# GpSimd's folds, sums and weight splits go to VectorE, and the norms around matrix multiplications are rebuilt

## The chip, the core and the metric

The kernel runs on one core of a Trainium2 chip. The metric is the time of one execution on the device in microseconds: the median of several runs. The profile is taken from one execution by the hardware profiler. TensorE (PE) multiplies matrices, VectorE (DVE) and ScalarE (ACT) work on elements, GpSimd (POOL) as well, and SyncE (SP) issues the DMAs of the weights.

## The reference

Three blocks work on one sequence of 256 tokens of width 1024, with 16 further tokens ahead of them in the first block. All arithmetic is float32.

```
h = concat([meta, x])                                  # 272 tokens
for i in range(2):                                     # first block
    f1 = swiglu(rmsnorm(h, g0), gate, up, down)
    h = h + 0.5 * rmsnorm(f1, g1)
    hn = rmsnorm(h, g2)
    m = neighborhood_attention(hn) if i == 0 else diff_attention(hn)
    h = h + rmsnorm(m, g3)
    f2 = swiglu(rmsnorm(h, g4), gate, up, down)
    h = h + 0.5 * rmsnorm(f2, g5)
h = h[:, 16:]                                          # second block
proj = rms_norm(h, g) @ w_in                           # u_pool, u_lru, u_gate
y = concat([pool_mixer(u_pool), rg_lru(conv(u_lru)) * gelu(u_gate)])
h = h + y @ w_out
h = h + square(relu(rms_norm(h, g) @ w_up)) @ w_down
h = h + sigmoid(rms_norm(h, g) @ w_ple_gate + b) * (p @ w_ple_proj)
h = rms_norm(h, g)
# third block: adaptive norm, short conv and window attention, w_out, then peer_ffn
# (16384 experts, top 16 of 8 heads) added to the stream
```

`rmsnorm(x, g)` is `x * rsqrt(mean(x*x) + 1e-6) * g`.

## The kernel before

The stream `h` lies with features on partitions: 8 tiles of 128 features, each with N = 272 or 256 columns of tokens. A float32 multiplication is made of three passes: each weight block and each input is split into a high part (`hi`, `zh`, `ah`: ACT, L66 and L269) and the rest (`lo`, `zl`, `al`: a subtraction), and TensorE adds hi·high, lo·high and hi·rest (L181, L182, L186).

Weights come in blocks of 128x1024. `Stream.use` hands the next block to a multiplication and splits the blocks that are to come: two ahead, three in the first part. A flag `gp` in the plan says whether VectorE or GpSimd makes `lo` (L67). GpSimd has the flag for most blocks of the mixing block (`w_in_2`, gates, pool, `w_ple_proj_2`, the first half of `w_out_2`) and for some of the third block.

`gemm_it` runs the outputs in groups of four tiles. For each group it goes over K in chunks of two tiles, 24 matmuls each, accumulating in PSUM banks: one bank for each output at N = 272, one for two outputs at N = 256. `evac` takes a group out of PSUM.

A norm is a sum over partitions: squares of 8 tiles are folded into one (`sq`), a matmul with a column of ones sums it (`ss_add`, L214), ACT and VectorE make the reciprocal root (`nsd`, `nv`, `ny`: `ss_chain`, `root`), and a matmul with the identity spreads it over all partitions (`ss_spread`, L244). There are two kinds.

- Behind a projection (`proj_post_it`): its output is squared and scaled by the gain (`fg`), and `update` adds `fg` times the spread root to `h` (tiles `ut`, two at a time from the third on, the add on GpSimd, L326).
- Ahead of a multiplication (`z_tile`, `z_after`): the input is split without its root, and the root is multiplied into the outputs of the multiplication, so its sum may come while the first group runs. `z_tile` makes `zh`, `zl` and the squares of two tiles and lets GpSimd fold them (L276, L278).

`update` and `z_tile` are called from the multiplication itself as its inputs come due. Each engine works its instructions off in the order in which they are issued here. The mixing block (`mixer_2`) runs its elementwise work from a generator that `gemm_it` steps once per chunk (`self.step`), beside the multiplications. The last stage, `peer`, streams 256 blocks of expert tables and keeps its GpSimd work.

Of the kernel before, what the change touches and what calls it, by code (L numbers as in the profile page):

```python
# [86 lines left out]
class Kern:  # L87
# [57 lines left out]
    def gemm_it(self, name, KT, groups, N, rhs, evac, after=None, tail=None):  # L145
# [3 lines left out]

        nc = self.nc  # L150
        per_bank = 1 if N > 256 else 2
        pending = None
        for og, g in enumerate(groups):
# [3 lines left out]
            else:  # L157
                banks = [self.bank2() for _ in range((g + 1) // 2)]
                outs = [banks[o // 2][:, o % 2] for o in range(g)]
            per = 8 // g  # L160
            for kc in range(0, KT, per):
# [4 lines left out]
                if pending is not None and kc:  # L166
                    next(after, None)
                    evac(*pending)
                    pending = None
                if after is not None and og == 0 and end:  # L170
                    next(after)
                order = [(k2, o) for k2 in range(min(per, KT - kc)) for o in range(g)]
                if kc and end:
                    order.sort(key=lambda x: (x[1] // per_bank, x[0], x[1]))
                late = []
                for n, (k2, o) in enumerate(order):
# [3 lines left out]
                    first = kt == 0 and (N > 256 or o % 2 == 0)  # L180
# [7 lines left out]
                    if tail is not None and end and og == len(groups) - 1 and (n + 1) * g % len(order) == 0:  # L188
                        b = (n + 1) * g // len(order) - 1
                        if (b + 1) % per_bank == 0:  # L190
                            tail(b // per_bank, outs)
                yield
            if og == 0 and after is not None:
                next(after)
# [8 lines left out]
    def gemm(self, *args, **kw):  # L203
        for _ in self.gemm_it(*args, **kw):
            pass

# [41 lines left out]
    def ss_rows(self, ss, N):  # L248
        return self.ss_spread(ss, self.ss_chain(ss, N), N)
# [12 lines left out]
    def z_tile(self, kt, g, c0, N):  # L262

        nc, gp = self.nc, self.nc.gpsimd
# [10 lines left out]
        if kt:  # L275
            gp.tensor_tensor(sq[:, 0:2, :N], sq[:, 0:2, :N], sq[:, p, :N], op=OP.add)  # L276
        if kt == 6:
            gp.tensor_tensor(sq[:, 0, :N], sq[:, 0, :N], sq[:, 1, :N], op=OP.add)  # L278

    def z_after(self, N):  # L280
# [3 lines left out]
        def after():  # L284
            yield
# [24 lines left out]
    def update(self, g, c0, N):  # L310
# [4 lines left out]
        def add(kt):  # L315
# [6 lines left out]
            else:  # L322
# [3 lines left out]
                self.nc.gpsimd.tensor_tensor(hk, hk, t, op=OP.add)  # L326
# [18 lines left out]
    def proj_post_it(self, name, KT, rhs, N, gpost, bias=None):  # L345

        nc, gp = self.nc, self.nc.gpsimd
# [5 lines left out]
        def piece(og, b, outs):  # L353
            per = 1 if N > 256 else 2
            for o in range(per * b, per * b + per):
                kt = 4 * og + o
                nc.scalar.activation(sq[:, kt, :N], outs[o], AF.Square,  # L357
                                     **({} if bias is None else {"bias": bias(kt)}))
            for o in range(per * b, per * b + per):
                kt = 4 * og + o  # L360
                if kt == 6 and N > 256:
# [1456 lines left out]
```

## Time and profile before

| | |
|---|---|
| median of 3 runs | 2502.68 us (2500.74 to 2504.39) |
| the profiled execution | 2512.54 us |
| its span | 2510.8 us |
| TensorE busy | 2366.9 us |
| VectorE busy | 1862.3 us |
| ScalarE busy | 1133.1 us |
| GpSimd busy | 516.6 us, of it 228.6 in the last stage (L1472) and 162.7 for `lo` (L67) |

The span is from the first to the last instruction on the core. Busy time is the time in which at least one instruction of the engine runs; matmuls overlap. The view of the cores gives the mean clock that TensorE was granted, where 1.00 is 2.4 GHz and 0.50 is 1.2 GHz, its two levels.

### The profile page before, as it was taken

How to read it: one execution, taken by the hardware profiler on the slowest of the kernel's cores; microseconds unless marked ns; L12 is line 12 of the kernel's file. 1: busy time of each engine (PE TensorE's matmuls, PEld its weight loads, DVE VectorE, ACT ScalarE, POOL GpSimd, SP SyncE). 2: the span in 40 equal slices, each digit the busy share in tenths (PEclk: the TensorE clock that was granted, in tenths of full speed). 3: DMA queues.
4: the chain of work that ended last, by engine and by line, in shares of the span. 5: the costliest groups of instructions: out<-in, count | busy, mean ns of one | idle time of the engine just before them, and what ended most of it. 6: DMA issues, size and time to landing. Idle time of an engine off the chain costs nothing.

```text
span 2510.8 us, 47982 instructions
## 1 busy us (share of the span) xinstructions
PE 2366.9 (94%) x19988; PEld 2296.5 (91%) x19988; DVE 1862.3 (74%) x2769; ACT 1133.1 (45%) x1509; POOL 516.6 (21%) x302
## 2 busy tenths in 40 slices
PE   8998998998999998998799989999889999899999
PEld 8998878998999978998789988999889999889999
DVE  7776657676776767777976565578989999999554
ACT  5444544444444454444555455454433334333443
POOL 0002002002001112003510015024445554553000
PEclk9998989998999988998899989899899999999999
DMA  6575414565557413666356543355444444444554
GB/s 216 176 248 200 164 51 133 184 227 178 176 192 266 147 64 126 201 230 203 114 168 204 194 152 123 128 177 185 146 141 152 152 150 153 143 135 152 187 188 147
DMA packets 114950, 418.79 MB, mean 167 GB/s; under 512 B 13086, under 2 KB 14382, under 8 KB 113708
## 3 DMA queue, kind: packets, MB, share of 16 engines
q1 hardware_dynamic: 113356, 406.46, 48.8%
q0 software_dynamic: 1376, 9.26, 1.0%
q8 instruction: 156, 2.56, 0.4%
q14 instruction: 62, 0.51, 0.1%
HBM read 414.62 MB, written 1.05 MB: 166 GB/s over the span
## 4 chain that ended last, share of the span: by engine, by line
PE 71%; DVE 18%; issue 4%; ACT 3%; POOL 2%; DMA 2%; DVEq 0%; SPq 0%; ACTq 0%; POOLq 0%
PE b L181 18%; PE b L186 17%; PE b L182 17%; DVE lo L67 5%; PE b L1555 4%; PE b L1553 4%; PE b L1554 4%; DVE zl L271 2%; DVE G L124 1%; DVE ob L1474 1%; ACT hi L66 1%; DMA raw<-in_dn 1%; PE b L1491 1%; DVE e L124 1%; PE b L214 1%
## 5 line engine op out<-in xcount | busy, mean ns | idle before, releaser
L67 DVE TENSOR_TENSOR lo<-raw,hi 128x1024 fp32r<-128x1024 f32 x658 | 895.9, 1371 | 421.3 <-ACT hi L66 420.3
L66 ACT ACTIVATE hi<-raw 128x1024 fp32r<-128x1024 f32 x722 | 754.8, 1056 | 841.1 <-PE b L186 412.4
L181 PE MATMUL b<-zh,hi 128*128 128x256 f32 (+1 forms) x3504 | 1013.0, 289 | 20.1 <-ACT zh L269 10.1
L182 PE MATMUL b<-zh,lo 128*128 128x256 f32 (+1 forms) x3504 | 1004.0, 287 | 17.6 <-DVE lo L67 13.5
L186 PE MATMUL b<-zl,hi 128*128 128x256 f32 (+1 forms) x3504 | 996.2, 286 | 14.6 <-DVE zl L271 14.6
L181 PEld LDWEIGHTS b<-zh,hi 128*128 128x128 f32 x3504 | 676.2, 193 | 28.5 <-ACT zh L269 11.3
L182 PEld LDWEIGHTS b<-zh,lo 128*128 128x128 f32 x3504 | 677.8, 193 | 20.1 <-DVE lo L67 14.8
L186 PEld LDWEIGHTS b<-zl,hi 128*128 128x128 f32 x3504 | 671.8, 193 | 17.4 <-DVE zl L271 17.3
L1555 PE MATMUL b<-zh,lo 128*128 128x256 f32 x1024 | 292.9, 286 | 2.6 <-DVE lo L67 2.6
L1553 PE MATMUL b<-zh,hi 128*128 128x256 f32 x1024 | 294.3, 287 | 0.0
L1554 PE MATMUL b<-zl,hi 128*128 128x256 f32 x1024 | 289.1, 282 | 0.0
L1472 POOL TENSOR_TENSOR oa<-e,gt 128x768 bf16<-128x768 bf16 x128 | 228.6, 1786 | 223.6 <-DVE e L124 196.9
L182 PE MATMUL b<-ah,lo 128*128 128x272 f32 (+1 forms) x960 | 271.1, 283 | 3.0 <-DVE lo L67 2.8
L181 PE MATMUL b<-ah,hi 128*128 128x272 f32 (+1 forms) x960 | 270.4, 282 | 0.0
L186 PE MATMUL b<-al,hi 128*128 128x272 f32 (+1 forms) x960 | 268.5, 282 | 0.0
L67 POOL TENSOR_TENSOR lo<-raw,hi 128x1024 fp32r<-128x1024 f32 x64 | 162.7, 2549 | 253.5 <-ACT hi L66 238.2
L1555 PEld LDWEIGHTS b<-zh,lo 128*128 128x128 f32 x1024 | 194.7, 190 | 6.5 <-DVE lo L67 4.6
L372 POOL TENSOR_TENSOR sq<-sq 128x272 f32<-128x272 f32 (+2 forms) x20 | 25.7, 1286 | 843.1 <-ACT sq L357 842.5
L1554 PEld LDWEIGHTS b<-zl,hi 128*128 128x128 f32 x1024 | 197.8, 193 | 0.0
L1553 PEld LDWEIGHTS b<-zh,hi 128*128 128x128 f32 x1024 | 195.0, 190 | 0.0
L182 PEld LDWEIGHTS b<-ah,lo 128*128 128x128 f32 x960 | 180.7, 188 | 4.4 <-DVE lo L67 4.4
L181 PEld LDWEIGHTS b<-ah,hi 128*128 128x128 f32 x960 | 180.7, 188 | 0.0
(374 smaller groups left out, 2663.2 us busy)
## 6 DMA issues: line engine op xcount, KB each, us to landing
raw<-in_gu SPq DMA_DIRECT2D x176, 512.0 KB, 4.2
raw<-in_peer_u SPq DMA_DIRECT2D x128, 512.0 KB, 3.3
raw<-in_peer_v SPq DMA_DIRECT2D x128, 512.0 KB, 3.3
raw<-in_dn SPq DMA_DIRECT2D x88, 512.0 KB, 4.7
raw<-in_w_adaT SPq DMA_DIRECT2D x48, 512.0 KB, 4.6
raw<-in_w_up SPq DMA_DIRECT2D x32, 512.0 KB, 4.2
raw<-in_w_down SPq DMA_DIRECT2D x32, 512.0 KB, 3.3
raw<-in_w_in SPq DMA_DIRECT2D x30, 512.0 KB, 3.4
```

What stands on the lines that cost most here:

```text
L66: nc.scalar.activation(hi[:, :width], raw, AF.Copy)
L67: (nc.gpsimd if gp else nc.vector).tensor_tensor(lo[:, :width], raw, hi[:, :width].bitcast(FT), op=OP.subtract)
L124: self.nc.vector.tensor_tensor(out, a, b, op=op)
L181: nc.tensor.matmul(outs[o], hi[:, w], xh, start=first, stop=False, skip_group_check=True)
L182: nc.tensor.matmul(outs[o], lo[:, w], xh, start=False, stop=False, skip_group_check=True)
L186: nc.tensor.matmul(out, a, b, start=False, stop=kt == KT - 1, skip_group_check=True)
L271: nc.vector.scalar_tensor_tensor(self.zl[:, k, :N], self.h[:, k, c0:c0 + N], self.gcol(g, k), self.zh[:, k, :N].bitcast(FT), op0=OP.mult, ...
L372: gp.tensor_tensor(sq[:, 0:w, :N], sq[:, 0:w, :N], sq[:, n:n + w, :N], op=OP.add)
L1472: nc.gpsimd.tensor_tensor(oa, e.unsqueeze(2).to_broadcast([128, 4, 3, 64]), gt[:, t0:t0 + 4].unsqueeze(3).to_broadcast([128, 4, 3, 64]), o ...
L1553: nc.tensor.matmul(dst, hi[:, w], ah[:, a], start=first, stop=False, skip_group_check=True)
L1554: nc.tensor.matmul(dst, hi[:, w], al[:, a], start=False, stop=False, skip_group_check=True)
L1555: nc.tensor.matmul(dst, lo[:, w], ah[:, a], start=False, stop=last, skip_group_check=True)
```

## The change

GpSimd is left with memsets, DMAs and its part of the last stage. The folds, the adds to `h`, the scaling of `e0` and all flagged splits ahead of the last stage are VectorE's. Besides:

- `z_tile` folds once, behind the last pair of tiles.
- `z_after`: the sum and root go from the end of the first group to the second chunk of the second group; the spread, and with it the first group's evacuation, to the chunk behind that.
- `proj_post_it`: each output is squared and folded as it is finished; the last output of a 256-column projection has a bank of its own; only two sums are made (tiles 0 and 7); the scalings of the last four outputs stand behind the sums.
- `warm(n)` issues n multiplications of the identity, read as bfloat16, into a bank that nobody reads: 6, 9 and 10 around the sums of a projection, 9 and 11 at two later norms (the second block's last and the third block's second). There are 190 in all.

```diff
     def gemm_it(...)
+                if tail is not None and og == len(groups) - 1:
+                    outs[g - 1] = self.bank()[:, :N]
...
                 if pending is not None and kc:
                     next(after, None)
-                    evac(*pending)
-                    pending = None
-                if after is not None and og == 0 and end:
-                    next(after)
+                    if kc >= 2 * per:
+                        evac(*pending)
+                        pending = None
...
             if og == 0 and after is not None:
-                next(after)
...
+    def warm(self, n):
+
+        b, x = self.bank(), self.ident.bitcast(BF)
+        for _ in range(n):
+            self.nc.tensor.matmul(b[:, :256], x[:, :128], x, start=True, stop=True)
...
     def ss_rows(self, ss, N):
-        return self.ss_spread(ss, self.ss_chain(ss, N), N)
+        y = self.ss_chain(ss, N)
+        self.warm(9)
+        rb = self.ss_spread(ss, y, N)
+        self.warm(11)
+        return rb
...
     def z_tile(self, kt, g, c0, N):
-        if kt:
-            gp.tensor_tensor(sq[:, 0:2, :N], sq[:, 0:2, :N], sq[:, p, :N], op=OP.add)
         if kt == 6:
-            gp.tensor_tensor(sq[:, 0, :N], sq[:, 0, :N], sq[:, 1, :N], op=OP.add)
+            for n in (2, 4, 6):
+                self.tt(sq[:, 0:2, :N], sq[:, 0:2, :N], sq[:, n:n + 2, :N], OP.add)
+            self.tt(sq[:, 0, :N], sq[:, 0, :N], sq[:, 1, :N], OP.add)
...
     def update(self, g, c0, N):
-                self.nc.gpsimd.tensor_tensor(hk, hk, t, op=OP.add)
+                self.tt(hk, hk, t, OP.add)
...
     def proj_post_it(self, name, KT, rhs, N, gpost, bias=None):
+        def tail(o, outs):
+            square(4 + o, outs[o])
+            if o < 3:
+                self.tt(sq[:, 0, :N], sq[:, 0, :N], sq[:, 4 + o, :N], OP.add)
             else:
-                st["ss"] = self.bank()
-                sums(0)
-                if N <= 256:
-                    sums(1), sums(6)
-                sums(7, True)
+                st["outs"] = outs
...
         yield from self.gemm_it(name, KT, [4, 4], N, rhs, evac, tail=tail)
-        self.rb = self.ss_rows(st["ss"], N)
+        outs = st["outs"]
+        self.warm(6)
+        ss = self.bank()
+        self.ss_add(ss, sq[:, 0, :N], N, True, False)
+        self.ss_add(ss, sq[:, 7, :N], N, False, True)
+        for o in range(2):
+            scaled(4 + o, outs[o])
+        y = self.ss_chain(ss, N)
+        for o in range(2, 4):
+            scaled(4 + o, outs[o])
+        self.warm(9)
+        self.rb = self.ss_spread(ss, y, N)
+        self.warm(10)
...
-                        nc.gpsimd.tensor_scalar(e0[:, j], e0[:, j], c[:, 0, j:j + 1], None, op0=OP.mult)
+                        nc.vector.tensor_scalar(e0[:, j], e0[:, j], c[:, 0, j:j + 1], None, op0=OP.mult)
...
-            gp = lambda i: True
-            add("w_in_2", 0, 4), add("w_in_2", 4, 5, gp=gp), add("gates_2", gp=gp), add("w_in_2", 9, gp=gp)
-            add("pool_2", gp=gp), add("w_ple_proj_2", gp=gp), add("w_out_2", gp=lambda i: i < 4)
+            add("w_in_2", 0, 4), add("w_in_2", 4, 6), add("gates_2"), add("w_in_2", 10)
+            add("pool_2"), add("w_ple_proj_2"), add("w_out_2")
```

VectorE's order at the first norm behind a projection (end of the first feed-forward part; `sq` folds, `fg` scalings, `nv` to `ny` the root, `ut` and `h` the update), before:

```order
L67 TENSOR_TENSOR lo<-raw,hi 128x1024 x3
L364 TENSOR_SCALAR fg<-b,vh 128x272 x2
L124 TENSOR_TENSOR sq<-sq 128x272
L364 TENSOR_SCALAR fg<-b,vh 128x272 x2
L236 TENSOR_SCALAR nv<-b 128x3
L225 RECIPROCAL ny<-nsd 128x3
L226 SCALAR_TENSOR_TENSOR na<-ny 128x3
L124 TENSOR_TENSOR na<-na,nv 128x3
L228 SCALAR_TENSOR_TENSOR ny<-na,ny 128x3
L124 TENSOR_TENSOR ut_2519<-fg,b 128x272
```

and now:

```order
L67 TENSOR_TENSOR lo<-raw,hi 128x1024 x3
L124 TENSOR_TENSOR sq<-sq 128x272 x3
L372 TENSOR_SCALAR fg<-b,vh 128x272 x2
L247 TENSOR_SCALAR nv<-b 128x3
L236 RECIPROCAL ny<-nsd 128x3
L237 SCALAR_TENSOR_TENSOR na<-ny 128x3
L124 TENSOR_TENSOR na<-na,nv 128x3
L239 SCALAR_TENSOR_TENSOR ny<-na,ny 128x3
L372 TENSOR_SCALAR fg<-b,vh 128x272 x2
L124 TENSOR_TENSOR ut_2547<-fg,b 128x272
L124 TENSOR_TENSOR h<-h,ut_2547 128x272
L124 TENSOR_TENSOR ut_2547<-fg,b 128x272
```

The three folds stand together, the scalings stand around the root's chain instead of ahead of it, and both adds to `h` follow `ut`.

VectorE's order a little later, where the next multiplication's fourth pair of tiles is split (`zl`) and the sum of its norm comes (`nv`), before:

```order
L271 SCALAR_TENSOR_TENSOR zl<-h,vt,zh 128x272 x2
L67 TENSOR_TENSOR lo<-raw,hi 128x1024
L271 SCALAR_TENSOR_TENSOR zl<-h,vt,zh 128x272 x2
L67 TENSOR_TENSOR lo<-raw,hi 128x1024 x2
L236 TENSOR_SCALAR nv<-b 128x3
L225 RECIPROCAL ny<-nsd 128x3
```

and now:

```order
L286 SCALAR_TENSOR_TENSOR zl<-h,vt,zh 128x272 x2
L67 TENSOR_TENSOR lo<-raw,hi 128x1024
L286 SCALAR_TENSOR_TENSOR zl<-h,vt,zh 128x272 x2
L124 TENSOR_TENSOR sq<-sq 128x544 x3
L124 TENSOR_TENSOR sq<-sq 128x272
L67 TENSOR_TENSOR lo<-raw,hi 128x1024 x4
L247 TENSOR_SCALAR nv<-b 128x3
L236 RECIPROCAL ny<-nsd 128x3
```

The folds are VectorE's, and four blocks' `lo` now stand ahead of `nv`, where there were two.

VectorE's order in the mixing block, from the root of its norm (`ul`, `up` are the projected parts, `xb` the convolution, `xl` the rest of its split), before:

```order
L124 TENSOR_TENSOR na<-na,nv 128x2
L228 SCALAR_TENSOR_TENSOR ny<-na,ny 128x2
L124 TENSOR_TENSOR ul<-b,r 128x2x256 x2
L970 SCALAR_TENSOR_TENSOR xb<-ul,vt,xb 128x256 x6
L124 TENSOR_TENSOR xl<-xb,xh 128x512
L970 SCALAR_TENSOR_TENSOR xb<-ul,vt,xb 128x256 x6
L124 TENSOR_TENSOR up<-b,r 128x2x256 x2
L124 TENSOR_TENSOR xl<-xb,xh 128x512
L124 TENSOR_TENSOR p_12880<-up 128x4x270
```

and now (from the same instruction):

```order
L124 TENSOR_TENSOR na<-na,nv 128x2
L239 SCALAR_TENSOR_TENSOR ny<-na,ny 128x2
L67 TENSOR_TENSOR lo<-raw,hi 128x1024
L124 TENSOR_TENSOR ul<-b,r 128x2x256 x2
L975 SCALAR_TENSOR_TENSOR xb<-ul,vt,xb 128x256 x6
L67 TENSOR_TENSOR lo<-raw,hi 128x1024
L124 TENSOR_TENSOR up<-b,r 128x2x256 x2
L124 TENSOR_TENSOR xl<-xb,xh 128x512
L975 SCALAR_TENSOR_TENSOR xb<-ul,vt,xb 128x256 x6
L67 TENSOR_TENSOR lo<-raw,hi 128x1024
L124 TENSOR_TENSOR xl<-xb,xh 128x512
```

The blocks' `lo` stand between the mixing work, which had none of them on this engine.

## Rows read from the trace of the kernel before

**Rows 1.** The page, part 1: busy us, share of span, instructions.

```profile
PE 2366.9 (94%) x19988; PEld 2296.5 (91%) x19988; DVE 1862.3 (74%) x2769; ACT 1133.1 (45%) x1509; POOL 516.6 (21%) x302
```

**Rows 2.** The view of the cores.

```profile
core 0: 2510.8 us, clock 0.960
```

**Rows 3.** TensorE's waits: for what, us in total, times, longest.

```profile
PE b L182 <- DVE lo L67: 17.2, 12, 4.6
PE b L186 <- DVE zl L271: 14.6, 13, 2.1
PE b L244 <- DVE ny L228: 12.3, 8, 3.6
```

**Rows 4.** TensorE's timeline, first norm (start, us, instruction, idle before).

```profile
208.84 0.29 PE L186 MATMUL b<-al,hi 128*128 128x272 f32 x1
210.51 1.66 PE L214 MATMUL b<-ones,sq 128*128 128x1 f32 x12 [1.39 <-DVE sq L124]
213.39 1.46 PE L244 MATMUL b<-ident,ny 128*128 128x128 f32 x6 [1.22 <-DVE ny L228]
216.41 0.59 PE L181 MATMUL b<-zh,hi 128*128 128x272 f32 x1 [1.56 <-ACT zh L269]
...
217.26 0.43 PE L182 MATMUL b<-zh,lo 128*128 128x272 f32 x1
217.48 0.43 PE L181 MATMUL b<-zh,hi 128*128 128x272 f32 x1
...
235.20 0.92 PE L214 MATMUL b<-ones,sq 128*128 128x1 f32 x6
```

**Rows 5.** VectorE's timeline, the same norm.

```profile
210.02 0.44 DVE L124 TENSOR_TENSOR sq<-sq 128x272 f32<-128x272 f32 x1 [0.68 <-POOL sq L372]
...
213.17 0.16 DVE L228 SCALAR_TENSOR_TENSOR ny<-na,ny 128x3 f32<-128x3 f32 x1
214.89 0.44 DVE L124 TENSOR_TENSOR ut<-fg,b 128x272 f32<-128x272 f32 x1 [1.56 <-PE b L244]
...
217.17 2.00 DVE L271 SCALAR_TENSOR_TENSOR zl<-h,vt,zh 128x272 fp32r<-128x272 f32 x2
...
226.53 2.38 DVE L67 TENSOR_TENSOR lo<-raw,hi 128x1024 fp32r<-128x1024 f32 x1
```

**Rows 6.** GpSimd's timeline, the same norm.

```profile
217.34 1.53 POOL L326 TENSOR_TENSOR h<-h,ut 128x544 f32<-128x544 f32 x1 [5.68 <-DVE ut L124]
```

**Rows 7.** Line L271 on VectorE, 971.75 to 973.2: ns min/median/max.

```profile
L271 DVE SCALAR_TENSOR_TENSOR zl<-h,vt,zh x2: 478/992/1507, 971.4 to 971.8; 128x256 fp32r<-128x256 f32 x2
```

**Rows 8.** Windows: length; busy us of PE, PEld, DVE, ACT, POOL; clock; DMA share; GB/s.

```profile
211.70:222.00 10.30, 7.52 (x34) 7.33 (x35) 7.77 (x16) 4.82 (x10) 3.65 (x3) 0.50 0.55 214
228.70:232.20 3.50, 1.46 (x9) 1.25 (x10) 3.50 (x4) 1.02 (x2) 2.25 (x2) 1.00 0.49 150
235.60:310.00 74.40, 74.40 (x551) 69.04 (x550) 45.83 (x107) 41.44 (x79) 0.57 (x1) 1.00 0.49 164
1172.00:1262.00 90.00, 66.87 (x477) 64.55 (x476) 79.69 (x89) 44.52 (x68) 49.01 (x23) 0.85 0.29 97
```

**Rows 9.** TensorE's timeline, the norm before the mixing block.

```profile
1166.06 3.58 PE L214 MATMUL b<-ones,sq 128*128 128x1 f32 x16 [4.13 <-POOL sq L372]
```

**Rows 10.** VectorE by form, 260 to 290.

```profile
L67 DVE TENSOR_TENSOR lo<-raw,hi 128x1024 fp32r<-128x1024 f32 x9 | 10.9, 1225 | 11.8 <-ACT hi L66 11.8
```

**Rows 11.** VectorE by form, mixing block, 1172 to 1262.

```profile
L271 DVE SCALAR_TENSOR_TENSOR zl<-h,vt,zh 128x256 fp32r<-128x256 f32 x8 | 9.4, 1211 | 0.3 <-ACT zh L269 0.3
...
L1000 DVE SCALAR_TENSOR_TENSOR rr<-th,rr 128x512 f32<-128x512 f32 x2 | 5.5, 2744 | 0.1
...
L228 DVE SCALAR_TENSOR_TENSOR ny<-na,ny 128x2 f32<-128x2 f32 x1 | 2.3, 2259 | 0.0
...
L1020 DVE SCALAR_TENSOR_TENSOR t<-t,rr 128x512 f32<-128x512 f32 x2 | 1.4, 688 | 0.7 <-ACT t L1018 0.7
```

**Rows 12.** GpSimd by form, the same stretch.

```profile
L67 POOL TENSOR_TENSOR lo<-raw,hi 128x1024 fp32r<-128x1024 f32 x15 | 37.6, 2521 | 31.3 <-ACT hi L66 31.3
```

More of the change, by code (lines that the diff above doesn't have):

```diff
@@ L159, in gemm_it @@
                 outs = [banks[o // 2][:, o % 2] for o in range(g)]
+                if tail is not None and og == len(groups) - 1:
+                    outs[g - 1] = self.bank()[:, :N]
+            unit = {}
+            for o in range(g):
+                alone = N > 256 or tail is not None and og == len(groups) - 1 and o >= g - 2
+                unit[o] = o if alone else o // 2 * 2
             per = 8 // g
@@ L187, in gemm_it @@
                         late = []
[L188 to L191, printed above, removed]
+                    if tail is not None and end and og == len(groups) - 1:
+                        u = [unit[x[1]] for x in order[n:n + 2]]
+                        if len(set(u)) == 2 or len(u) == 1:
+                            for t in range(u[0], o + 1):
+                                tail(t, outs)
                 yield
             if og == 0 and after is not None:
-                next(after)
                 if N > 256:
@@ L262, in z_tile @@
     def z_tile(self, kt, g, c0, N):
-        nc, gp = self.nc, self.nc.gpsimd
+        nc = self.nc
         if kt % 2:
@@ L351, in proj_post_it @@
         st = {}
[L353 to L361, printed above, removed]
-                    self.tt(sq[:, 0, :N], sq[:, 0, :N], sq[:, 6, :N], OP.add)
-                if bias is None:
-                    nc.vector.tensor_scalar(fg[:, kt, :N], outs[o], gpost(kt), None, op0=OP.mult)
-                else:
-                    nc.vector.tensor_scalar(fg[:, kt, :N], outs[o], bias(kt), gpost(kt), op0=OP.add, op1=OP.mult)
@@ L368, in sums, with square @@
-        def sums(n, last=False):
-            self.ss_add(st["ss"], sq[:, n, :N], N, n == 0, last)
-        def fold(n, w):
-            gp.tensor_tensor(sq[:, 0:w, :N], sq[:, 0:w, :N], sq[:, n:n + w, :N], op=OP.add)
-        def tail(b, outs):
-            if N > 256:
-                piece(1, b, outs)
-                if b < 2:
-                    fold(4 + b, 1)
-            else:
-                piece(1, b, outs)
-                if b == 0:
-                    fold(4, 2)
+        def square(kt, x):
+            nc.scalar.activation(sq[:, kt, :N], x, AF.Square, **({} if bias is None else {"bias": bias(kt)}))
@@ L385, in evac @@
             if og == 0:
-                for b in range(4 if N > 256 else 2):
-                    piece(0, b, outs)
-                fold(2, 2)
-                if N > 256:
-                    fold(1, 1)
-            else:
-                st["ss"] = self.bank()
-                sums(0)
-                if N <= 256:
-                    sums(1), sums(6)
-                sums(7, True)
-        yield from self.gemm_it(name, KT, [4, 4], N, rhs, evac, tail=tail)
-        self.rb = self.ss_rows(st["ss"], N)
+                for o in range(4):
+                    square(o, outs[o])
+                    scaled(o, outs[o])
```

19 lines of the change are left out of this document (13 added, 6 removed).

## The prediction

> **What bounds the kernel now.** I read the page's list of engines first: TensorE is busy 94% of the span, VectorE 74%, GpSimd 21% [rows 1]. A kernel like this is shortened in two ways: take away places where TensorE stands idle, or keep its clock up. The row of the cores gives a mean granted clock of 0.960 [rows 2]. With two levels (1.2 and 2.4 GHz, 0.5 and 1.0 in the profile), 0.04 lost is 8% of the span, about 200 us, at half clock. TensorE's waits come next: its largest here are for VectorE's lower halves `lo` (17.2 us), `zl` (14.6) and the norms' root `ny` (12.3 in 8 places) [rows 3]. They sit at norms and in the mixing block, which are the places the change touches.
>
> The first norm shows the pattern (TensorE's timeline, [rows 4]). The last matmul starts at 208.84; the sums of squares start only at 210.51, because a square is folded late; the root takes until 213.39; the next matmuls start at 216.41. From there matmuls are 0.22 us apart (217.26, 217.48): half clock. The windows say the same: 0.50 over 211.7 to 222, and TensorE fully busy at 1.00 over 235.6 to 310 [rows 8]. In between comes a second hole: over 228.7 to 232.2 TensorE works 1.46 of 3.5 us while VectorE is busy all 3.50. Another fall to 0.50 follows.
>
> VectorE is late there for one reason that the rows show directly. The same `zl` instruction took 478 ns and, next in line, 1507 ns [rows 7]; the long one ran under a GpSimd add. On VectorE's timeline `zl` x2 is 2.00 us and `lo` 2.38 us [rows 5], against 1225 ns for `lo` where GpSimd is idle [rows 10]. A GpSimd add of a pair of tiles takes 1.53 us [rows 6], and holds VectorE's two-input work for about that long. In the mixing block a 128x2 instruction, 0.16 us elsewhere [rows 5], took 2259 ns while GpSimd made `lo` of 2521 ns [rows 11, 12].
>
> The Trainium skill, SBUF — State Buffer, section Who interferes with whom, says that a VectorE instruction with two SBUF inputs contends with a GpSimd one that reads SBUF. The trace agrees (478 and 1507 ns).
>
> **The change part by part.** The profiled execution took 2512.5 us, 0.4% more than the median of 2502.7. I make the sum against it and apply the difference to the median.
>
> *A. The five norms that feed a next multiplication (ends near 209, 381, 591, 802, 963).* Before the root: the three folds go to VectorE (0.44 us each) right behind the last `lo`, and the two scalings that stood ahead of them go behind the sums. VectorE's 210.02 fold, which waited 0.68 us for GpSimd [rows 5], now ends about 209.8, so the sums begin about 0.6 us earlier. The root's chain is unchanged. The spread, 1.46 us at half clock, would be 0.7 to 0.9 at full clock if the dummies hold it: -0.6. Together -1.2; for 256 columns half of the sums' records go as well, -1.5. Five places: -6.
>
> After the root I walk VectorE's queue from the first `ut` (214.89 is zero), in the new order and at undisturbed prices: two `ut`/`h` pairs of one tile 1.65 (four instructions of 0.44, each starting a little inside the one before); each later pair of tiles `ut` 0.63 and `h` 0.67, 1.3; each `zl` 0.42 to the next start; each `lo` 1.14. So `zl` 0, 1 are done at 3.8, 2, 3 at 5.95, a `lo` at 7.1, 4, 5 at 9.2, a `lo` at 10.4, 6, 7 at 11.2. Before, the last `zl` was done near 16.4. TensorE starts at +1.55, stands 0.9 us for the first `zl` and some tenths for later ones, and at 0.123 us a matmul ends its fourth chunk of 24 at about +14.65. Before, the sums behind that chunk started at 235.20 [rows 4], which is +20.3. The gain is 5.7 there. In the other four places the same distance, read in the same way, is 19.0, 20.3, 18.9 and (256 columns) 17.7, against 14.65 and 13.85: the five make -23.8. All of A by this walk is -30. I take -25, since it leaves out every small semaphore gap and small clock falls. Bounds: -12, if half is lost, to -30.
>
> *B. The norm before the mixing block, and the block.* The sums wait 4.13 us there for GpSimd's fold [rows 9]; but ACT's squares ahead of it are late too, behind a weight load, so only about 1.2 goes. In the 90 us behind it VectorE is busy 79.69 and GpSimd 49.01 [rows 8]. There a `zl` is 1211 ns against 478, `rr` of L1000 2744 against 688 for L1020, which has the same form and size, `ny` 2259 against 160 [rows 11]. These three kinds (8, 2 and 1 of them) give 5.9 + 4.1 + 2.1 = 12 us too much; the other long forms (`xb`, the scan, `pd`, `xl`, `th`, `pc`, `na`, `rr` of L998 and L1022, one `lo`), set against equal sizes in the same way, give about 21: 33. What comes to VectorE is 15 and a half `lo` by 1.14 (GpSimd's 15 in [rows 12] and a half-width one), 17.7, folds 2.2 and three `h` 1.8: 21.7. VectorE's work falls by about 11.5. VectorE is the wait there (10 of 90 us idle, a few of it closable), so -16 with some of its idle time; with the 1.2, B is -17. Bounds: -6, if the new `lo` stand in front of what TensorE needs, to -24.
>
> *C. Other places.* First norm, the entry of the expanding multiplication behind the mixer, the end of the second block, the third block's norms: each has a shorter hole of the same kind, -5 in all (0 to -9).
>
> *D. What it costs.* Dummies: 25 at each of six projections and 20 at two other norms. A 128x256 matmul is at most 0.21 us (0.22 x 256/272 at half clock), half of that at full clock. Nine take 1.0 us at full clock against the root's wait of 1.2 to 1.6, ten 1.1 against 1.56 [rows 4]: covered. The last output's own bank, and the later evacuation of the first group, shift the ring of PSUM banks: with 272 columns the second group's last output waits for the first group's first output in three feed-forward gates, 0.5 to 1.5 us each: 0 to +4. In every pre-norm (9 of them) the root of the sums now stands on VectorE behind the `lo` of that chunk, as the order shows; it is done 0 to 0.4 us after the spread could start: +2. Scalings of e0 and remaining folds: VectorE is busy 45.83 of 74.40 us in the steady stretch [rows 8], so they are hidden; if that cover failed, 16 scalings by the 0.44 of a one-tile instruction [rows 5] would be 7. D is +2 to +4; I take +3. GpSimd's few loads of tables lose only work that stood between them; SP's loads are unchanged.
>
> Sum: -25 - 17 - 5 + 3 = -44; 2512.5 becomes 2468.5, and the median 2502.7 becomes about **2459**.
>
> **Rivals.**
> *The dummies don't hold the clock.* For: they depend on waits being as long as they were; at half clock six, nine and ten of them last 1.3, 1.9 and 2.1 us, longer than the holes, about +1 in each of eight places. Against: TensorE is at 1.00 wherever it is fed [rows 8]. The spread's gain and about half of the 23.8 go: -44 + 3 + 12 + 8 = -21, **2482**.
>
> *VectorE's single queue takes the place of GpSimd's lane.* In the mixer `lo` now stand between `ul`, `xb` and `up`, and each waits for ACT's `hi`; what stands behind waits as well. Speaking for it: VectorE at 89% there. If B is nothing and half of A goes: -44 + 17 + 12 = -15, **2488**.
>
> *VectorE becomes the bound: slower.* Mechanism: the long rows are not GpSimd's doing, and don't shorten. Then 21.7 us are added to 79.69 in 90, of which 10.3 idle can take some: +11 to +22; at each norm three `h` of 0.7 stand ahead of `zl`, +1.8 x 5 = 9; D +3; sums earlier -6. About +22, **2525**. It decides from the point where less than about a third of the 33 us comes back. Against it: 478 and 1507 ns for one form, back to back [rows 7]. The Trainium skill speaks for this case: Perfetto Trace Analysis, section Optimizing Scalar/DVE Operations, says that work may well be given to GpSimd when VectorE is saturated. The same section warns that the two share a read port, so that this may not help; the rows here bear out the warning.
>
> *More than forecast.* The walk holds in full and the mixer gives 24: -44 - 5 - 7 - 4 = -60, **2443**.
>
> *No change,* because the gains in single places are given back to weight loads: TensorE's queue of weights would then be the bound. The steady stretch, busy throughout [rows 8], speaks against it. **2502**.
>
> **Numbers.** Likeliest (2446 to 2472) 0.62; more 0.08; dummies 0.13; queue 0.10; slower 0.04; no change 0.03. Predicted 2459; the range reaches from 2440, below which half of the "more" case lies, to 2486, which takes in the dummies' case: about 0.8. The measurement can tell 0.2% (5 us): faster 0.93, same 0.03, slower 0.04.
>
> **What would show it.** Right: no `zl` over 0.6 us before the last stage; `lo` at 1.2; a granted clock well above 0.50 in the first 10 us behind the sums; no hole for `zl` in the third chunk; sums behind the fourth chunk, or its end, about 15 us after `ut`; the mixing stretch 15 us shorter. Wrong: 0.50 over the dummies; a wait of TensorE for `ny` or `lo` that is larger than in [rows 3]; VectorE busy without a gap in the mixer and no shorter; a wait of TensorE's second group for a bank.

## The result, and the profile after

The changed kernel took 2476.4 us in the median of four runs (2463.3 to 2482.3), against 2503.5 for the kernel before in the same comparison: a ratio of 0.9871, interval 0.9838 to 0.9905. The gain is 27 us by these medians and 32 by the ratio; the prediction had 44. The measured median lies 17 us above the predicted 2459: inside the stated range (2440 to 2486), outside its likeliest part (2446 to 2472), and nearer to the 2482 of the rival in which the dummies don't hold the clock. The total alone therefore doesn't say which account holds; the runs below do. A second set of six runs gave 2474.6 and 0.9868 (0.9845 to 0.9892). The profiled execution is the fastest of these ten, 2463.3 us with a span of 2461.5, which is 49 us under the profiled execution before. So the pair of profiles shows more gain than the runs have, and I come back to that.

The page's engines and the view of the cores:

```profile
PE 2352.2 (96%) x20162; PEld 2277.8 (93%) x20162; DVE 1854.0 (75%) x2897; ACT 1134.9 (46%) x1509; POOL 319.9 (13%) x180
```

```profile
core 0: 2461.5 us, clock 0.978
```

GpSimd fell from 516.6 to 319.9 us, but VectorE did not rise: 1854.0 us against 1862.3 [rows 1], with 128 more instructions. What it took over cost it about as much as it got back. The mean granted clock rose from 0.960 to 0.978 [rows 2].

TensorE's waits:

```profile
PE b L187 <- DVE lo L67: 22.3, 11, 4.7
PE b L676 <- ACT sq L1236: 8.5, 1, 8.5
...
PE b L907 <- ACT sq L893: 5.8, 2, 5.5
...
PE b L191 <- DVE zl L286: 4.1, 8, 0.8
...
PE b L255 <- DVE ny L239: 1.3, 6, 0.2
```

The waits for `zl` fell from 14.6 to 4.1 us, those for `ny` from 12.3 to 1.3 [rows 3]. Those for `lo` did not fall (17.2 before). Two are large and stand in a place of their own: 8.5 us for the squares of the third block (L1236) and 5.8 us, 5.5 of them at once, for the last squares of the second (L893).

The first norm, which [rows 4] showed before; TensorE, with the last matmul of the projection first and the first one of the next multiplication's fifth chunk last, then VectorE:

```profile
208.44 0.29 PE L191 MATMUL b<-al,hi 128*128 128x272 f32 x1
...
209.62 1.50 PE L225 MATMUL b<-ones,sq 128*128 128x1 f32 x12 [0.22 <-DVE sq L124]
...
212.34 0.84 PE L255 MATMUL b<-ident,ny 128*128 128x128 f32 x6 [0.21 <-DVE ny L239]
...
214.74 0.39 PE L186 MATMUL b<-zh,hi 128*128 128x272 f32 x1 [0.46 <-ACT zh L284]
...
228.04 0.28 PE L191 MATMUL b<-zl,hi 128*128 128x272 f32 x1
228.17 0.29 PE L186 MATMUL b<-zh,hi 128*128 128x272 f32 x1
```

```profile
213.22 0.44 DVE L124 TENSOR_TENSOR ut<-fg,b 128x272 f32<-128x272 f32 x1
...
216.26 0.91 DVE L286 SCALAR_TENSOR_TENSOR zl<-h,vt,zh 128x272 fp32r<-128x272 f32 x2
...
222.66 1.22 DVE L67 TENSOR_TENSOR lo<-raw,hi 128x1024 fp32r<-128x1024 f32 x1
223.79 0.91 DVE L286 SCALAR_TENSOR_TENSOR zl<-h,vt,zh 128x272 fp32r<-128x272 f32 x2
```

The sums start 1.18 us behind the projection's last matmul (before 1.67); most of that is dummies now, and 0.22 us is idle instead of 1.39. The spread takes 0.84 us at full clock (before 1.46). `zl` x2 is 0.91 us (before 2.00), `lo` 1.22 (before 2.38) [rows 5]. Four chunks of 24 matmuls lie between 214.74 and 228.17, so the fourth chunk is through 15.0 us after the first `ut` (213.22); before, it took 20.3 us, up to the sums at 235.20 [rows 4].

Windows: the first norm, the mixing block and the end of the second block (columns as in [rows 8]):

```profile
200.00:235.00 35.00, 33.18 (x267) 31.63 (x266) 26.78 (x50) 17.37 (x29) 1.73 (x3) 1.00 0.63 218
1143.00:1220.00 77.00, 66.04 (x536) 64.38 (x535) 71.69 (x113) 48.20 (x72) 0.00 (x0) 0.97 0.38 133
1427.00:1442.00 15.00, 9.04 (x46) 7.63 (x45) 7.81 (x18) 4.92 (x11) 1.18 (x3) 0.54 0.29 105
```

At the first norm there is no half clock at all. In the mixing block it is 0.97 (before 0.85 [rows 8]). At the end of the second block it is 0.54, the lowest of the three. VectorE's forms in the mixing block (columns as in [rows 11]):

```profile
L67 DVE TENSOR_TENSOR lo<-raw,hi 128x1024 fp32r<-128x1024 f32 x18 | 21.8, 1218 | 2.7 <-ACT hi L66 2.7
...
L286 DVE SCALAR_TENSOR_TENSOR zl<-h,vt,zh 128x256 fp32r<-128x256 f32 x8 | 3.5, 479 | 0.0
...
L1005 DVE SCALAR_TENSOR_TENSOR rr<-th,rr 128x512 f32<-128x512 f32 x2 | 1.4, 692 | 0.1
...
L239 DVE SCALAR_TENSOR_TENSOR ny<-na,ny 128x2 f32<-128x2 f32 x1 | 0.2, 161 | 0.0
```

`zl` is 479 ns instead of 1211, `rr` of L1005 692 instead of 2744, `ny` 161 instead of 2259 [rows 11], with 18 `lo` at 1218 ns among them. The long rows were GpSimd's doing.

To see where the time went I took the start of ACT's split of the same weight block in both traces (the 722 splits come in the same order, but for one block inside the second stretch that changes places with the gates'), and read the length of four stretches:

| stretch (blocks) | before | after | second trace of it |
|---|---|---|---|
| first block, to the norm before the mixer (0 to 330) | 1155.7 | 1125.6 | 1129.8 |
| that norm, mixing block, entry of the expansion (330 to 360) | 129.7 | 107.3 | 107.0 |
| rest of the second block, third block (360 to 465) | 359.1 | 365.7 | 372.2 |
| last stage (465 to the last) | 845.9 | 842.1 | 844.2 |

The first two stretches gained 52.5 us (48.6 in the second trace). The third lost 6.6, in the second trace 13.1. The last stage is not touched by the change; it differs by 2.1 us between the two traces of one kernel, and I don't count its 3.8 us as a gain.

### The profile page after: what moved, and what is told of

Its sections match the earlier page's. It is cut to its first block, busy times and chain, and to the rows that moved or that the text cites. A ratio compares the mean times of both kernels' runs of the same rounds, so it can differ in the third digit from the quotient of the medians.

```text
span 2461.5 us, 48284 instructions
## 1 busy us (share of the span) xinstructions
PE 2352.2 (96%) x20162; PEld 2277.8 (93%) x20162; DVE 1854.0 (75%) x2897; ACT 1134.9 (46%) x1509; POOL 319.9 (13%) x180
## 4 chain that ended last, share of the span: by engine, by line
PE 75%; DVE 17%; issue 4%; ACT 2%; DMA 1%; POOL 1%; DVEq 0%; SPq 0%; ACTq 0%; POOLq 0%
PE b L186 19%; PE b L187 19%; PE b L191 19%; DVE lo L67 6%; PE b L1562 4%; PE b L1560 4%; PE b L1561 4%; DVE G L124 1%; DVE ob L1481 1%; PE b L1498 1%; ACT hi L66 1%; DVE e L124 1%; DMA raw<-in_dn 1%; DVE ut L124 1%; PE b L225 1%
## 5 line engine op out<-in xcount | busy, mean ns | idle before, releaser
L67 DVE TENSOR_TENSOR lo<-raw,hi 128x1024 fp32r<-128x1024 f32 (+1 forms) x690 | 918.0, 1341 | 430.1 <-ACT hi L66 429.2
L186 PE MATMUL b<-zh,hi 128*128 128x256 f32 (+1 forms) x3504 | 1000.6, 286 | 11.9 <-ACT hi L66 8.4
L187 PE MATMUL b<-zh,lo 128*128 128x256 f32 (+1 forms) x3504 | 991.8, 283 | 19.4 <-DVE lo L67 16.7
L191 PE MATMUL b<-zl,hi 128*128 128x256 f32 (+1 forms) x3504 | 985.4, 283 | 4.5 <-DVE zl L286 4.1
L187 PEld LDWEIGHTS b<-zh,lo 128*128 128x128 f32 x3504 | 666.9, 190 | 22.1 <-DVE lo L67 18.6
L186 PEld LDWEIGHTS b<-zh,hi 128*128 128x128 f32 x3504 | 665.5, 190 | 20.2 <-ACT hi L66 9.1
L191 PEld LDWEIGHTS b<-zl,hi 128*128 128x128 f32 x3504 | 661.3, 190 | 7.0 <-DVE zl L286 7.0
L1562 PEld LDWEIGHTS b<-zh,lo 128*128 128x128 f32 x1024 | 194.7, 190 | 5.4 <-DVE lo L67 3.7
L1561 PEld LDWEIGHTS b<-zl,hi 128*128 128x128 f32 x1024 | 198.0, 193 | 0.0
L1560 PEld LDWEIGHTS b<-zh,hi 128*128 128x128 f32 x1024 | 195.2, 191 | 0.0
L191 PEld LDWEIGHTS b<-al,hi 128*128 128x128 f32 x960 | 180.3, 189 | 0.0
L67 POOL TENSOR_TENSOR lo<-raw,hi 128x1024 fp32r<-128x1024 f32 x32 | 84.0, 2626 | 161.9 <-ACT hi L66 161.9
```

What stands on the lines that cost most here:

```text
L67: (nc.gpsimd if gp else nc.vector).tensor_tensor(lo[:, :width], raw, hi[:, :width].bitcast(FT), op=OP.subtract)
L186: nc.tensor.matmul(outs[o], hi[:, w], xh, start=first, stop=False, skip_group_check=True)
L187: nc.tensor.matmul(outs[o], lo[:, w], xh, start=False, stop=False, skip_group_check=True)
L191: nc.tensor.matmul(out, a, b, start=False, stop=kt == KT - 1, skip_group_check=True)
L1560: nc.tensor.matmul(dst, hi[:, w], ah[:, a], start=first, stop=False, skip_group_check=True)
L1561: nc.tensor.matmul(dst, hi[:, w], al[:, a], start=False, stop=False, skip_group_check=True)
```

## The experiments

Each was compared with the kernel before. Medians of the kernel before in these comparisons are 2507 to 2510 us.

**The change once more, for its spread.** No edit.

> The changed kernel once more, unaltered. If its spread (2463 to 2482) belongs to it, the times fall in the same band, median 2470 to 2480, and the runs with a lower mean granted clock are the longer ones (0.970 against 0.978: 1.6% of the span more at half clock, about 40 us, of which half is lost: +15 to +20). If the first fast execution was the odd one, all lie within 0.3% of 2477.

2474.6 us (2471.8 to 2481.9). The times fall in the same band. The clock goes with part of it: the fastest two runs have a mean of 0.977 and 0.976, the other four 0.971 to 0.973. The trace shows one place plainly: behind the 8.5 us wait in the third block, 34 us of the second trace and of the first, and then a steady stretch of the first:

```profile
1515.60:1549.60 34.00, 28.02 (x151) 23.88 (x152) 15.13 (x46) 14.52 (x33) 0.00 (x0) 0.55 0.14 47
```

```profile
1512.40:1546.40 34.00, 27.74 (x204) 24.21 (x205) 17.89 (x48) 16.09 (x35) 0.00 (x0) 0.80 0.22 77
1260.00:1300.00 40.00, 40.00 (x356) 40.00 (x355) 27.25 (x28) 23.41 (x23) 0.00 (x0) 1.00 0.59 201
```

The same work runs at 0.55 there and 0.80 here. The half clock lasted 30.7 us in one execution and 13.7 in the other, behind a wait of the same length.

**Without the dummies.**

```diff
     def warm(self, n):
...
+        return
```

> The changed kernel without its 190 dummy multiplications; nothing of the result's computation is left out. If the dummies hold the clock: the granted clock falls behind six projections again, mean clock 0.962 to 0.966, and the time rises by 12 to 25 us. If the clock is held because the holes are shorter and the dummies are only in the way: mean clock as it is, time the same or 5 us less.

2488.8 us (0.9911, 0.9889 to 0.9933): 14 us slower than the change, and each of its seven runs is longer than each of the change's second set (2483.3 and more, against 2481.9 and less). The mean clock is 0.960 to 0.966. TensorE's waits for `ny`, and two windows, a steady one and the first norm:

```profile
PE b L253 <- DVE ny L237: 10.0, 8, 1.5
```

```profile
1276.00:1316.00 40.00, 40.00 (x342) 40.00 (x341) 25.31 (x27) 21.98 (x22) 0.00 (x0) 1.00 0.62 202
216.00:226.00 10.00, 7.66 (x43) 7.34 (x44) 9.03 (x21) 6.16 (x11) 0.00 (x0) 0.66 0.55 217
```

The clock falls again behind the projections (0.66 at the first norm). That was the first expectation. The window at 1276 (the expanding multiplication) shows something else, for below: 342 matmuls in 40.00 us, with granted clock 1.00, where the change makes 356 (window 1260 above).

**Only the move.** The kernel before with its norms as they were and no dummies:

```diff
-            gp.tensor_tensor(sq[:, 0:2, :N], sq[:, 0:2, :N], sq[:, p, :N], op=OP.add)
+            self.tt(sq[:, 0:2, :N], sq[:, 0:2, :N], sq[:, p, :N], OP.add)
...
-                self.nc.gpsimd.tensor_tensor(hk, hk, t, op=OP.add)
+                self.tt(hk, hk, t, OP.add)
```

and all other folds, e0 and the plan in the same way.

> The kernel before, with its norms as they were and no dummies, but with GpSimd's folds, adds, scaling and splits ahead of the last stage on VectorE. If GpSimd's hold on VectorE's long rows is the main cause: mixing block about 18 us shorter, the holes for zl gone, third block 6 us longer, median about 2480. If the rebuilt norms and the dummies carry most: only the mixing block gains, median 2490 to 2497.

2485.0 us (0.9913, 0.9889 to 0.9937), the same as the change without dummies. So the move alone is about 22 us of the 33, and the rebuilt norms bring nothing that the medians tell until the dummies are in them. No run has dummies in the norms as they were, so whether the dummies need the rebuilding stays open. The waits for `zl`:

```profile
PE b L186 <- DVE zl L271: 0.2, 1, 0.2
```

The holes for `zl` are gone (14.6 us before). The first three stretches of the table take 1139.6, 109.5 and 367.5 us: 16 and 20 shorter than before, and 8 longer. The 8.5 us wait of the third block is there as well: it belongs to the move.

**GpSimd back at the norms.** The adds to `h` and the folds ahead of a multiplication on GpSimd; splits, rebuilt norms and dummies as changed.

```diff
-                self.tt(hk, hk, t, OP.add)
+                self.nc.gpsimd.tensor_tensor(hk, hk, t, op=OP.add)
...
-            for n in (2, 4, 6):
-                self.tt(sq[:, 0:2, :N], sq[:, 0:2, :N], sq[:, n:n + 2, :N], OP.add)
...
+            gp.tensor_tensor(sq[:, 0:2, :N], sq[:, 0:2, :N], sq[:, p, :N], op=OP.add)
...
```

> The changed kernel with the adds to h (from the third tile on) and the folds of the norms ahead of a multiplication back on GpSimd; splits, rebuilt norms and dummies as changed. If GpSimd's hold on zl and lo, and its slower adds, made the holes behind the five norms: zl of 1 us and more comes back, with a hole for the last zl of about 2 us, and from the first ut to the end of the fourth chunk it takes 17 to 19 us instead of 14.5: +12 to +22 over six norms. If the dummies and the earlier sums made that gain: 0 to +5.

2504.7 us (0.9993, 0.9968 to 1.0018): about 30 us slower than the change, more than expected, and no gain left against the kernel before. VectorE at the first norm, TensorE's waits for `zl`, and the window of the first norm:

```profile
227.82 2.49 DVE L286 SCALAR_TENSOR_TENSOR zl<-h,vt,zh 128x272 fp32r<-128x272 f32 x2
```

```profile
PE b L191 <- DVE zl L286: 23.6, 21, 2.0
```

```profile
200.00:235.00 35.00, 30.02 (x233) 27.81 (x233) 27.85 (x37) 16.21 (x26) 12.40 (x10) 1.00 0.57 198
```

This is the clearest of the runs. At the first norm the dummies do hold the clock: 1.00 over the window. And it does not help: TensorE makes 233 records there, against 267 in the change, since VectorE is late with `zl` again (2.49 us for the last two), and TensorE waits 23.6 us for it in all, more than the 14.6 of the kernel before. From the first `ut` to the end of the fourth chunk the five norms take 18.9 to 20.1 us, a little more than expected, and the first stretch 1157.4 us, as in the kernel before (1155.7). A clock held up brings TensorE only sooner to the same wait here.

**GpSimd back in the mixing block.**

```diff
-            add("w_in_2", 0, 4), add("w_in_2", 4, 6), add("gates_2"), add("w_in_2", 10)
-            add("pool_2"), add("w_ple_proj_2"), add("w_out_2")
+            gp = lambda i: True
+            add("w_in_2", 0, 4), add("w_in_2", 4, 6, gp=gp), add("gates_2", gp=gp), add("w_in_2", 10, gp=gp)
+            add("pool_2", gp=gp), add("w_ple_proj_2", gp=gp), add("w_out_2", gp=lambda i: i < 4)
```

> The changed kernel with the mixing block's splits (w_in_2 from its fifth block, gates, pool, w_ple_proj_2, first half of w_out_2) back on GpSimd; folds, adds, norms and dummies as changed. If GpSimd's hold on VectorE's two-input rows is what the mixing block gained from: the long rows come back (zl above 1 us, ny above 1 us), the stretch from the norm to the expanding multiplication is 14 to 20 us longer, and the median with it. If the rebuilt norms made the gain: 0 to 4 us.

2493.5 us (0.9934, 0.9900 to 0.9968), 19 slower. VectorE's forms there:

```profile
L286 DVE SCALAR_TENSOR_TENSOR zl<-h,vt,zh 128x256 fp32r<-128x256 f32 x8 | 7.6, 1003 | 0.0
...
L237 DVE SCALAR_TENSOR_TENSOR na<-ny 128x2 f32<-128x2 f32 x1 | 2.0, 2031 | 0.0
```

The long rows are back, and blocks 330 to 360 take 120.6 us against 107.0 in the second trace of the change: 13.6 of the 22.4 that this stretch gained. The traced execution is the slowest of this kernel's seven (2515.0 us), and where the other 5 us of the 19 lie is not shown.

**Third block: w_in_3's splits on GpSimd, then w_out_3's as well.**

```diff
-            add("w_in_3"), add("w_out_3")
+            add("w_in_3", gp=lambda i: i > 5), add("w_out_3")
```

> The changed kernel with the splits of w_in_3 from its seventh block on given back to GpSimd. If the 8.5 us wait at the end of that multiplication comes from VectorE and ScalarE waiting for each other in turn (a root-free score waits behind lo, lo behind hi, hi behind the exponentials of the last score), it falls to 2 to 4 us and the time by 4 to 7. If VectorE's longer rows beside GpSimd cost the same, the place takes as long as now: 0 to -1.

2482.9 us (0.9891, 0.9866 to 0.9916): no gain that can be told. The wait is 6.7 us, which misses the expected 2 to 4. The trace shows why: the `lo` that stand between the last scores are already those of w_out_3, prefetched, and they were still VectorE's. So the next run gave back both (`add("w_out_3", gp=lambda i: i < 4)` too):

> The changed kernel with both sets of the third block's splits back on GpSimd (w_in_3 from the seventh block, w_out_3's first four). The run with w_in_3's alone still had three lo of w_out_3 on VectorE between the scores and a wait of 6.7 us. If VectorE and ScalarE waiting for each other in turn is the cause, the wait for the squares falls to 2 to 4 us, as before the change, and the time is 4 to 10 us under the unaltered one. If it is something in the norms: wait 6 us or more, no gain.

2470.7 us (0.9832, 0.9797 to 0.9867): 4 us under the change, which these runs do not tell apart from it. The wait, as before the change:

```profile
PE b L676 <- ACT sq L1236: 2.6, 1, 2.6
```

**Third block: exponentials a step later.** Nothing on GpSimd; the wait is taken away by the order instead.

```diff
                 nc.vector.tensor_scalar(ng, mx, -1.0, None, op0=OP.mult)
-                for j in range(2):
-                    nc.scalar.activation(sl[:, j, ks[j]], ...Exp...)
-                nc.scalar.activation(zs, ng, AF.Exp, bias=snk[:, h:h + 1])
...
                 def rest():
+                    for j in range(2):
+                        nc.scalar.activation(sl[:, j, ks[j]], ...Exp...)
+                    nc.scalar.activation(zs, ng, AF.Exp, bias=snk[:, h:h + 1])
+                    yield None
```

> The changed kernel, nothing back on GpSimd, but in the third block each score's exponentials are issued one step later, behind the next score's maximum, and its normalisation one step behind that. If the two engines wait for each other in turn (about 4.3 us a step, against 2.7 of matmuls), the step falls to ScalarE's 2.4 us, the wait for the squares from 8.5 to under 4 us, and the time by 4 to 10 us. If VectorE's own work fills the place, the wait stays at 7 us or more.

2475.6 us (0.9836, 0.9799 to 0.9874; 2457.8 to 2485.7). The wait:

```profile
PE b L676 <- ACT sq L1236: 0.7, 1, 0.7
```

The wait for the squares is 0.7 us; 3.6 us of it came back at the next root. VectorE's maxima there now follow each other 2.86 us apart, where the change has them 4.35 us apart (its rows stand further below):

```profile
1519.99 0.17 DVE L1254 TENSOR_SCALAR ng<-mx 128x2 f32<-128x2 f32 x1
...
1522.85 0.17 DVE L1254 TENSOR_SCALAR ng<-mx 128x2 f32<-128x2 f32 x1
```

Blocks 360 to 465 take 358.9 us, as in the kernel before. The mechanism is shown; the time is not told apart from the change's by these runs, since the intervals overlap.

**Norms ahead of a multiplication as before.** Sums at the end of the first group, spread and evacuation a chunk earlier.

```diff
                     next(after, None)
-                    if kc >= 2 * per:
-                        evac(*pending)
-                        pending = None
+                    evac(*pending)
+                    pending = None
...
             if og == 0 and after is not None:
+                next(after)
...
-            add("w_in_2", 0, 4), add("w_in_2", 4, 6), add("gates_2"), add("w_in_2", 10)
+            add("w_in_2", 0, 4), add("w_in_2", 4, 5), add("gates_2"), add("w_in_2", 9)
```

The last two lines put the mixing block's weights back into the order in which they are then used.

> The changed kernel with the sums of the norms ahead of a multiplication back at the end of the first group, and the spread and the first group's evacuation a chunk earlier, as before the change. If the later place serves the root (no wait for VectorE's folds), going back costs 0.3 to 1 us at each of nine places: +3 to +8. If the later evacuation is what lengthened the wait at the end of the second block (5.5 us against 3.8), that wait shortens by about 2 and the rest is even: -3 to 0.

2470.0 us (0.9838, 0.9809 to 0.9868; 2465.2 to 2471.9). The last squares of the second block:

```profile
PE b L907 <- ACT sq L893: 4.2, 3, 3.8
```

5.5 became 3.8 (4.2 with two small ones, against 5.8). Going back costs nothing; if anything it is 5 us better, so the later place did not serve. The intervals touch, and I leave it at that.

**Dummies doubled.** `for _ in range(2 * n)`.

> The changed kernel with each set of dummies doubled (380 in all). If dummies beyond the wait delay what stands behind them, every doubled set costs 0.6 to 1.2 us at full clock where the wait is filled already (sums, spread): +10 to +20 in eight places. If the waits still have room, or a fuller clock pays for them: -3 to +4.

2484.3 us (0.9908, 0.9875 to 0.9940), 10 us slower than the change by the medians, the low end of the first expectation; the intervals overlap a little. The trace shows 3 us of it at the five norms, 0.6 us each. Numbers as chosen about fill the waits there; more of them stand in the way.

**Both edits together, then with dummies where the clock still fell.** The first is the later exponentials with the earlier sums.

> The changed kernel with both edits that shortened a wait in the traces so far: exponentials of the third block's scores one step later, and the sums of the norms ahead of a multiplication back at the end of the first group. If the two gains are separate places (8.5 us of wait and its half clock in the third block; 2 to 4 us at the mixing block and the end of the second), they add: median 2460 to 2467, 0.5% under the changed kernel. If the time is held by something common to all runs: 2470 or more.

2471.5 us (0.9849, 0.9815 to 0.9882): they didn't add to anything that can be told from the change. The second adds dummies at two waits:

```diff
-        self.warm(6)
+        self.warm(24 if name == "dn11" else 6)
...
         if kt == 6:
+            if cols is not None:
+                self.warm(34)
```

> As the kernel before it in this list, with 18 more dummies ahead of the sums before the mixing block and 34 ahead of the last sums of the second block, where TensorE waits 2.5 and 4.2 us and its clock still falls. If dummies hold the clock wherever the wait covers them: no half clock at these two places (10 to 17 us of it less), 3 to 7 us shorter. If the fall there has other reasons, or the dummies outlast the wait: same or up to 3 us longer.

2460.6 us (2455.3 to 2466.9), ratio 0.9808 (0.9778 to 0.9837). This beats both kernels: 50 us under the one before and 14 under the change, whose interval (0.9845 to 0.9892) it does not touch. The end of the second block without these dummies and with them:

```profile
1427.00:1442.00 15.00, 11.24 (x59) 10.47 (x59) 7.38 (x15) 5.84 (x11) 1.18 (x3) 0.65 0.42 141
```

```profile
1427.00:1442.00 15.00, 14.52 (x111) 13.25 (x110) 8.87 (x16) 7.86 (x14) 1.18 (x3) 0.89 0.34 108
```

0.65 becomes 0.89 there: some 7 us less at half clock in these 15, worth half of that. Blocks 420 to 435, which hold this place, take 60.1 us against 63.1. At the other place, before the mixing block, the traces show no gain: the sums stand 4.3 us behind the projection's last matmul, without the added dummies 3.8. So 3 of the 11 us between the two medians are accounted for, the intervals of these two overlap a little, and the rest is open. In the two traces a further 6.5 us lie in the third block (blocks 435 to 450), where both kernels do the same.

## Why the prediction was right or wrong

**A, the five norms: right, between the walk and what I took.** The walk along VectorE's queue gave -30, I took -25. At the first norm the fourth chunk is through 15.0 us after `ut`, where the walk had 14.65; at the other four it takes 15.0, 14.9, 14.9 and 14.1 (walk: three times 14.65, then 13.85). From the last matmul of the projection to the last one of the fourth chunk the five take 125.1 us before and 97.6 now (97.2 in the second trace). The runs divide these 27.5 us: 109.8 with the move alone, 102.3 with the rebuilt norms and no dummies, 121.2 with all of it but GpSimd back at the norms. So a VectorE without GpSimd beside it is most of it, and the dummies about 5. The doubt whether they hold the clock is settled by the window at 1.00, but with GpSimd at the norms they and the rebuilding together bring 4 of the 27.5. The first stretch as a whole gained 30.1 us in the profiled pair, 25.9 in the second trace.

**B, norm and mixing block: right in mechanism for the block, -22.4 for -17; the norm's 1.2 us did not come.** The rows that I read as too long went back to their undisturbed length, and VectorE's busy time over blocks 330 to 360 fell from 107.2 to 94.9 us, 12.3 against the forecast 11.5. The rest of the gain is time in which VectorE stood idle: I had put it at some 5 us, and it was about 10. The norm's sums still wait 3.9 us (4.13 before), so almost nothing of the 1.2 went. The reason is the one I named, ACT's squares behind a weight's split:

```profile
1136.77 1.67 PE L225 MATMUL b<-ones,sq 128*128 128x1 f32 x8 [3.88 <-DVE sq L124]
```

```profile
1132.92 1.06 ACT L66 ACTIVATE hi<-raw 128x1024 fp32r<-128x1024 f32 x1 [1.32 <-PE b L216]
1133.88 1.19 ACT L368 ACTIVATE sq<-b 128x256 f32<-128x256 f32 x4
```

In the second trace that split waits 1.38 us for the transfer of its weight block:

```profile
1137.04 1.06 ACT L66 ACTIVATE hi<-raw 128x1024 fp32r<-128x1024 f32 x1 [1.38 <-DMA raw<-in_w_in]
```

**C, other places, -5: this step failed.** "Each has a shorter hole of the same kind" is wrong in sign: blocks 360 to 465, which hold two of the four places (the end of the second block and the third block), lost 6.6 and 13.1 us. I had the mechanism among the rivals (VectorE's single queue in place of GpSimd's lane), but put it into the mixing block, where it did not happen. It happened in the third block. ACT's and VectorE's timelines of the changed kernel there (`sl` the exponentials, `hi` and `lo` a weight's split, `ng` a score's maximum):

```profile
1507.91 0.40 ACT L1256 ACTIVATE sl<-sl,ng 128x128 f32<-128x128 f32 x1 [2.23 <-DVE z L124]
...
1508.99 1.04 ACT L66 ACTIVATE hi<-raw 128x1024 fp32r<-128x1024 f32 x1
1512.26 0.40 ACT L1256 ACTIVATE sl<-sl,ng 128x128 f32<-128x128 f32 x1 [2.23 <-DVE z L124]
...
1516.27 1.23 ACT L1236 ACTIVATE sq<-y 128x512 f32<-128x512 f32 x2 [1.89 <-DVE y L124]
```

```profile
1507.65 0.17 DVE L1254 TENSOR_SCALAR ng<-mx 128x2 f32<-128x2 f32 x1
...
1510.06 1.23 DVE L67 TENSOR_TENSOR lo<-raw,hi 128x1024 fp32r<-128x1024 f32 x1 [1.39 <-ACT hi L66]
...
1512.00 0.17 DVE L1254 TENSOR_SCALAR ng<-mx 128x2 f32<-128x2 f32 x1
```

Read the two together: `ng` at 1507.65 frees the exponentials at 1507.91 (the view names `z`, VectorE's short add right behind `ng`); `hi` stands behind them at 1508.99; `lo` waits for `hi` and starts at 1510.06; the next score's maximum stands behind `lo`, with `ng` at 1512.00; the next exponentials at 1512.26. Each step of 4.35 us goes round both engines, with neither busy for all of it. Before, `lo` was on a third engine and the ring was open. The squares come at 1516.27, TensorE has waited 8.5 us, and the clock falls for 13.7 or 30.7 us. Taking `lo` away (2.6 us of wait) or letting the exponentials lag (0.7) both open it. The second wait that grew, at the end of the second block, comes from the later evacuation of the first group, which I had priced among the ring of banks only: 5.5 us with it, 3.8 with the sums as before. Behind it the dummies of that norm ran at half clock, ahead of the spread of r1, as the rival on dummies had it for all its places:

```profile
1438.80 2.32 PE L216 MATMUL b<-ident 128*128 128x256 bf16 x11
```

Of the third stretch's loss, blocks 420 to 435 with this wait lost 2.7 us (2.9 in the second trace) and blocks 435 to 450 with the ring 5.3 (11.7).


**D, costs, +3: about right as far as it shows.** TensorE's waits name no bank of PSUM, and blocks 22 to 44 of the first feed-forward part take 66.0 us in both kernels. `ny` behind `lo` costs 1.3 us in all. The dummies fit their waits at the five norms. What I had not seen is the price above, at the end of the second block.

**The sum.** -30, -22, +7 and a little from the last stage make the -49 of the profiled pair; the forecast -44 had two errors, A and B too small and C with the wrong sign, that nearly cancel there, and that is luck. By their ratios the runs show -32 and -33. The rival without a held clock (2482), to which the median lies nearer, is ruled out by the runs without dummies: they are 14 us slower still. The difference between pair and runs is in what varies between executions: the profiled execution after was the fastest run, the one before (2512.5) among the slower. The half clock behind the 8.5 us wait is one cause that the traces show, some 6 us. How the rest is shared out stays open.

The page of the Trainium skill that spoke against the change (Perfetto Trace Analysis, Optimizing Scalar/DVE Operations) names the choice rightly: VectorE was 93% busy in the mixing block afterwards (71.69 of 77 us) and yet the stretch was shorter, since what GpSimd did in parallel had cost VectorE as much as it saved. Its caution decided, not its rule.

## What to carry to other kernels

Look at a small instruction's longest duration before you give work to a second engine: a 128x2 row of 2.26 us beside one of 0.16 tells what the helper costs. When work moves from a third engine onto one of two that already pass results to each other, write down who waits for whom in one loop step, because the queue may close into a ring. And keep a clock up only where the engine behind it can deliver: the dummies were worth about 14 us with VectorE freed, and with GpSimd back at the norms they and the rebuilding together gained nothing.

## What the runs showed of the hardware

TensorE has stretches of some 100 to 200 us in which every matmul is further apart while the granted clock reads 1.00: 342 records against 356 in 40 us above, with no gap (about 0.118 us from start to start for 256 columns, else 0.113). The same blocks (360 to 420) take 171.4 us there and 165.5 in the change. Eight of the fourteen traces have such stretches in steady multiplications, one to four of them; the kernel before, both traces of the change and three others have none. Four of the five executions with two or more of them are the slowest runs of their kernels, 10 to 22 us above the median, which speaks for something that varies between executions; no kernel was traced both with and without, so that is not shown, and I found no cause in the traces. One execution's profile is therefore good for a mechanism and not for a difference of 10 us.

GpSimd held up more than VectorE's two-input work. In the kernel before, `rr` of L998, which has one input and two constants, took 0.42 us with GpSimd idle and 2.60 us while GpSimd made `lo` (three of them from 1229.93 on, 7.91 us); after the change both of its kind take 0.42:

```profile
1224.59 0.42 DVE L998 TENSOR_SCALAR rr<-rr 128x512 f32<-128x512 f32 x1
...
1230.21 2.60 DVE L998 TENSOR_SCALAR rr<-rr 128x512 f32<-128x512 f32 x1
```
